# A hybrid decoder layer on one core: h2's first sum alone in the norm's chain, the other sums behind it, and the first gate and up blocks in another order

## The chip, the cores and the metric

One core of a Trainium2 chip runs the whole program. The metric is device microseconds of one launch. The engines are named as in the profile: PE is TensorE (matmuls; PEld its weight loads), DVE is VectorE, ACT is ScalarE, POOL is GpSimd, SP is SyncE, which issues most of the DMAs.

## What is computed

One layer of a decoder with T = 512 tokens and D = 1024, in float32: three token mixers in parallel, their gated sum times `w_out`, a norm and the residual, and then a SwiGLU feed-forward part with DFF = 2816. The change lies where the two meet:

```python
x = x + rmsnorm(mixed @ w_out[l], norm_mix_post[l])
h = rmsnorm(x, norm_ffn_pre[l])
f = (jax.nn.silu(h @ ffn_w_gate[l]) * (h @ ffn_w_up[l])) @ ffn_w_down[l]
x = x + rmsnorm(f, norm_ffn_post[l])
```

The second `h` is called h2 below.

## The kernel before

**Split matmuls.** Each float32 operand is kept as a high part H (a copy by ScalarE that rounds) and a low part L (the rest, a subtraction by VectorE). A product of two operands is three matmuls: H with H, H with L, L with H.

**Seven products for eight.** h2 and the weights of gate and up are cut into 2 x 2 quarters (h2: first or second 256 tokens by first or second half of D; a weight: halves of D by halves of its columns). A block of a gate or up result takes seven products instead of eight. Their left operands are the quarters a11, a12 and a22 of h2 and four sums of quarters: s1 = a22 - a21 (with the kernel's signs), s2 from s1 and a11, s4 from s2 and a12, s3 = a11 - a21. Their right operands are quarters and sums of quarters of the weight. The products accumulate into four PSUM banks, pa, pd and pc by name: pa takes a11, s2, s3 and a22 one after the other, pc takes s1 and s4, pd takes a12. In between, `copy` saves the states c11, c12 and c22.

**Blocks.** The columns of DFF stand as 22 tiles of 128, 11 in each half; `chunks` cuts the 11 into six blocks n = 0 to 5, of two tiles each and one in the last. For every n there is a `Block` for gate ("g", ends in silu into `ga`) and one for up ("u", multiplies into `ga`). A product is 24 matmuls of 128x256 (12 in block 5). `first` is the product with a11, `second` with a12, `middle` those with s1, s2, s4 and s3, `last` the one with a22. `first` and `second` need the first 256 tokens alone.

**Weight sums.** For n in `FF_SUMMED` (0, 4 and 5) the sums of quarters are made in DRAM ahead of time: `behind` takes the next job off a list (`todo`), a copy on SP's queue (L180) and then an accumulating DMA on POOL's queue (L181). The jobs of n = 0 come first, then those of the down weights, then those of n = 4 and 5. Two sums of a weight start from another sum, so their copy waits for that sum's accumulate. The other blocks (n = 1, 2, 3) load four raw quarters (`fetch`, L1017) and sum them on VectorE (`plus`, L1030). Every weight operand is then cast by ScalarE (L1042, "wH") and subtracted by VectorE (L1043, "wL").

**Buffers.** Raw weights go through `avail`, three buffers "raw_ff" and, until n = 4, four more named "fraw". Two halves of one slot carry the names "two_...", so a "two_fraw" in a row is one of these.

**The chain to the sums.** The tokens stand in four row tiles t = 0 to 3. For each, `post_norm` adds to the residual x, `pre_norm` makes hn (L303; its factor by a pow on POOL, L280), PE transposes hn (L306, "h2t"), and `put_h2` copies the transposed half to af (L916) and splits it: `Part.put` has ScalarE copy the high part (L904) and VectorE subtract the low one (L905). With t = 2 and 3, the second 256 tokens, `sums_h2` (L931 to L938) makes all five parts s1, s2, s3, a22 and s4 of that row tile, 128x512 each, at once. The chain of the last two row tiles runs in high priority.

**Order.** A scheduler orders the instructions of each engine by the place in the program and by `tc.high_priority`; weights (loads, casts, sums) are moved ahead by LEAD = 400. Block 0 runs `first` and `second` of gate and up; block 1 of gate likewise (L1133 on), and then the `middle` of g0, of u0, and what is left. So six products stand ahead of the first one with s1. `a11.put` and `a12.put` (L981, L982) split the finished `ga` of a group of tiles for the down projection.

## Time and profile before

| | us |
|---|---|
| runs shown | 836.03, 837.03, 838.95 |
| median | 837.03 |
| profiled execution, its time | 835.83 |
| its span | 833.9 |
| PE busy | 805.1 (97%) |
| DVE busy | 553.2 (66%) |
| ACT busy | 387.4 (46%) |
| POOL busy | 110.3 (13%) |

The profile's times count from the span's start; the span is the part of an execution in which an instruction runs, 1.9 us less than the time. Busy time is the time in which at least one instruction of an engine runs. Matmuls overlap in the rows of a timeline: a row shows when a matmul starts and how long it is in the engine, and the next starts before it ends. "[3.04 <-DVE h2s L905]" behind a row says that the engine was idle for 3.04 us before it and that the instruction at L905 that wrote h2s released it. PEclk is the clock granted to PE, as a share of full speed.

### The profile page before, as it was taken

The page shows a single profiled execution, that of the slowest core. Times are in us where ns is not written, and L with a number is a line of the kernel's source. Part 1 is how long each engine was busy: PE and PEld are TensorE (multiplying, and loading weights), DVE is VectorE, ACT ScalarE, POOL GpSimd, SP SyncE. Part 2 cuts the span into 40 slices and gives each one's busy share as a digit, 9 for nine tenths or more (in the row PEclk, how much of TensorE's full clock was granted, in tenths as well). Part 3 has the DMA queues.
Part 4 walks back from the last instruction along what each step waited for, and adds up shares of the span by engine and source line. Part 5 has one row for each costly group of instructions (what it writes and reads, how often), then busy time and mean ns, then how long its engine had stood idle before and what let it go on. Part 6 is the DMA issues. An engine that isn't in the chain of part 4 may idle for free.

```text
span 833.9 us, 12187 instructions
## 1 busy us (share of the span) xinstructions
PE 805.1 (97%) x4778; PEld 716.4 (86%) x4778; DVE 553.2 (66%) x792; ACT 387.4 (46%) x588; POOL 110.3 (13%) x109
## 2 busy tenths in 40 slices
PE   5999999999999999999999999899999999989995
PEld 5888998889888877888888889899999999778884
DVE  4639967776477644433455685779787756987666
ACT  5445324555365432323343484255545544655552
POOL 2210023211111002322221000100000000000001
PEclk9999999999999999999999999899999999999998
DMA  8574557662776985998756368975730554566772
GB/s 303 151 153 109 144 158 167 159 158 66 205 200 130 295 231 127 251 217 221 190 155 177 119 209 207 263 175 142 193 109 27 162 155 140 187 193 235 219 259 106
DMA packets 114811, 147.35 MB, mean 177 GB/s; under 512 B 5425, under 2 KB 89154, under 8 KB 114370
## 3 DMA queue, kind: packets, MB, share of 16 engines
q1 hardware_dynamic: 96066, 124.56, 46.8%
q0 software_dynamic: 18688, 22.02, 17.8%
q8 instruction: 37, 0.61, 0.3%
q14 instruction: 20, 0.16, 0.1%
HBM read 142.36 MB, written 48.23 MB: 229 GB/s over the span
## 4 chain that ended last, share of the span: by engine, by line
PE 88%; DVE 5%; DMA 3%; ACT 1%; issue 1%; SPq 0%; POOL 0%; DVEq 0%; POOLq 0%; ACTq 0%
PE p L1186 9%; PE paffn_w_up L1049 7%; PE paffn_w_gate L1049 7%; PE pga L244 5%; PE pgb L244 5%; PE pgc L244 5%; PE ow L255 5%; PE pcffn_w_up L1049 3%; PE pcffn_w_gate L1049 3%; PE mv L255 3%; PE gv L255 3%; PE pya L244 3%; PE mq L244 3%; PE pu L244 3%; PE pyb L244 3%; PE mk L244 3%
## 5 line engine op out<-in xcount | busy, mean ns | idle before, releaser
L1178 DVE TENSOR_TENSOR wL_p<-raw_p,wH_p 128x1024 fp32r<-128x1024 f32 (+1 forms) x42 | 47.2, 1131 | 21.3 <-ACT wH_p L1177 21.1
L1177 ACT CAST wH_p<-raw_p 128x1024 fp32r<-128x1024 f32 (+1 forms) x42 | 41.0, 980 | 41.2 <-PE p L1186 13.8
L1186 PE MATMUL p<-wH_p,qs 128*128 128x512 f32 x176 | 54.7, 390 | 0.3 <-ACT two_c_u L1241 0.3
L1186 PE MATMUL p<-wH_p,a 128*128 128x512 f32 x132 | 41.3, 392 | 2.6 <-ACT wH_p L1177 2.6
L181 POOL DMA_DIRECT2D sum_d<-in_ffn_w_down_dram x24 | 21.3, 887 | 156.0 <-DMA sum_d<-in_ffn_w_down_dram 87.6
L1043 DVE TENSOR_TENSOR wL_ffn_w_up<-raw_ff,wH_ffn_w_up 128x1024 fp32r<-128x1024 f32 (+1 forms) x26 | 28.1, 1080 | 19.4 <-ACT wH_ffn_w_up L1042 19.3
L1186 PEld LDWEIGHTS p<-wH_p,qs 128*128 128x128 f32 x176 | 33.0, 188 | 7.5 <-ACT two_c_u L1241 0.7
L1042 ACT CAST wH_ffn_w_up<-raw_ff 128x1024 fp32r<-128x1024 f32 (+1 forms) x26 | 24.2, 932 | 32.6 <-issue 9.1
L1049 PE MATMUL pcffn_w_gate<-h2s,wH_ffn_w_gate 128*128 128x256 f32 x176 | 33.9, 291 | 3.0 <-DVE h2s L905 3.0
L280 POOL TENSOR_TENSOR rs_pf<-ms_pf,half 128x1 f32<-128x1 f32 x4 | 3.7, 921 | 231.7 <-DVE ssq_pf L277 224.0
L1186 PE MATMUL p<-wL_p,qs 128*128 128x512 f32 x88 | 34.2, 389 | 0.0
L1049 PE MATMUL paffn_w_up<-h2s,wH_ffn_w_up 128*128 128x256 f32 x176 | 33.9, 292 | 0.0
L1049 PE MATMUL paffn_w_gate<-h2a,wH_ffn_w_gate 128*128 128x256 f32 x176 | 33.3, 287 | 0.0
L1049 PE MATMUL paffn_w_up<-h2a,wH_ffn_w_up 128*128 128x256 f32 x176 | 32.9, 284 | 0.4 <-DVE c22ffn_w_up L1085 0.4
L1049 PE MATMUL paffn_w_gate<-h2s,wH_ffn_w_gate 128*128 128x256 f32 x176 | 32.8, 284 | 0.2 <-DVE h2s L905 0.2
L1042 ACT CAST wH_ffn_w_gate<-raw_ff 128x1024 fp32r<-128x1024 f32 (+1 forms) x26 | 24.2, 935 | 18.5 <-PE paffn_w_up L1049 6.5
L181 POOL DMA_DIRECT2D sum_ffn_w_gate<-in_ffn_w_gate_dram x12 | 12.5, 1038 | 152.9 <-DMA sum_ffn_w_gate<-sum_ffn_w_gate 86.6
L1049 PE MATMUL pcffn_w_up<-h2s,wH_ffn_w_up 128*128 128x256 f32 x176 | 32.4, 283 | 0.0
L1186 PEld LDWEIGHTS p<-wH_p,a 128*128 128x128 f32 x132 | 24.6, 188 | 8.4 <-ACT wH_p L1177 3.5
L1049 PEld LDWEIGHTS pcffn_w_gate<-h2s,wH_ffn_w_gate 128*128 128x128 f32 x176 | 28.7, 199 | 3.2 <-DVE h2s L905 3.2
L1043 DVE TENSOR_TENSOR wL_ffn_w_gate<-raw_ff,wH_ffn_w_gate 128x1024 fp32r<-128x1024 f32 (+1 forms) x26 | 27.7, 1076 | 4.4 <-ACT wH_ffn_w_gate L1042 4.2
L1042 ACT CAST wH_ffn_w_gate<-two_fraw 128x1024 fp32r<-128x1024 f32 x16 | 16.8, 1048 | 28.5 <-DVE two_fraw L1030 13.0
(406 smaller groups left out, 2647.3 us busy)
## 6 DMA issues: line engine op xcount, KB each, us to landing
sum_d<-in_ffn_w_down_dram POOLq DMA_DIRECT2D x20, 512.0 KB, 7.5
raw_p<-sum_d SPq DMA_DIRECT2D x20, 512.0 KB, 4.1
raw_p<-in_ffn_w_down_dram SPq DMA_DIRECT2D x15, 512.0 KB, 3.7
raw_ff<-in_ffn_w_gate_dram SPq DMA_DIRECT2D x12, 512.0 KB, 4.6
sum_d<-in_ffn_w_down_dram SPq DMA_DIRECT2D x10, 512.0 KB, 5.4
sum_d<-sum_d SPq DMA_DIRECT2D x10, 512.0 KB, 5.8
two_fraw<-in_ffn_w_up_dram SPq DMA_DIRECT2D x10, 512.0 KB, 4.8
sum_ffn_w_gate<-in_ffn_w_gate_dram POOLq DMA_DIRECT2D x8, 512.0 KB, 7.1
```

The lines of the kernel that those rows point to most:

```text
L181: nc.gpsimd.dma_start(dst, second, accum_op=ALU.add)
L244: PE.matmul(ps, lhsT=w[:, k, f * P:(f + 1) * P], rhs=m(k0 + k, lo, hi), start=n == 0 and i == 0, stop=n == len(W) - 1 and i == len(seq) - 1)
L255: PE.matmul(ps, lhsT=m(k0 + k, lo, hi), rhs=w[:, k, c0:c1], start=first and n == 0 and i == 0, stop=last and n == len(W) - 1 and i == len( ...
L280: pows.append(G.tensor_tensor(rs, ms, half[:, 0:1], op=ALU.pow))
L1042: S.copy(h, r)
L1043: V.tensor_tensor(l, r, h.bitcast(F32), op=ALU.subtract)
L1049: PE.matmul(self.ps[b][:, f, :], lhsT=w[:, k, f * P:(f + 1) * P], rhs=X.t[:, z, k, :], start=start and f == 0 and k == 0 and n == 0, stop= ...
L1177: S.copy(h, w)
L1178: V.tensor_tensor(l, w, h.bitcast(F32), op=ALU.subtract)
L1186: PE.matmul(ps[j], lhsT=X.part(z, k, j), rhs=w_[:, k - lo_, :], start=start and k == 0 and i == 0, stop=k == KH - 1 and i == 2, skip_group ...
```

## The change

- **Sums of h2.** `sums_h2` makes s1 alone, per row tile. The sums s2, s4, s3 and the part a22 come in `more_sums_h2`, called once behind the loop over the row tiles and without its priority, each for all 256 tokens (128x1024).
- **More in front.** In block 1 `first` and `second` of up run too before the first product with s1: eight products instead of six. There are six extra raw buffers instead of four; two are given back ahead of n = 4.
- **Alternation.** `middle` becomes a generator `steps`, with a stop behind each product. The steps of g0 and u0 run in turn, then those of g1 and u1 (g1 one ahead).
- **Sums of block 4.** `FF_SUMMED` loses 4, so block 4 loads raw quarters and sums on VectorE. `last` takes one job off the list per block, not two.
- **Banks.** PSUM banks are taken from a list and given back (pd behind `second`, pa and pc behind `last`) instead of turning.
- **a12.** The puts of a12's first two groups stand behind block 5 instead of behind blocks 1 and 3.

```diff
-FF_SUMMED = (0, 4, 5)
+FF_SUMMED = (0, 5)
...
     def sums_h2(c):
-        a11, a12, a21, a22 = (af[i, j][:, :, c * P:(c + 1) * P] for i in range(2) for j in range(2))
         if c == 0:
-            for n in ("s1", "s2", "s3", "a22", "s4"):
-                part[n] = Part(f"h2{n}")
+            part["s1"] = Part("h2s1")
             af["s"] = slot([P, 4, TH], "h2fs")
-        s_ = af["s"][:, :, c * P:(c + 1) * P]
+        a21, a22, s_ = (af[i][:, :, c * P:(c + 1) * P] for i in ((1, 0), (1, 1), "s"))
         V.tensor_tensor(s_, a22, a21, op=ALU.subtract)
         part["s1"].put(s_, c)
+
+    def more_sums_h2():
+        a11, a12, a21, a22 = (af[i, j] for i in range(2) for j in range(2))
+        s_ = af["s"]
+        for n in ("s2", "s4", "s3", "a22"):
+            part[n] = Part(f"h2{n}")
         V.scalar_tensor_tensor(s_, s_, -1.0, a11, ALU.mult, ALU.subtract)
-        part["s2"].put(s_, c)
+        part["s2"].put(s_)
+        V.scalar_tensor_tensor(a12, s_, -1.0, a12, ALU.mult, ALU.subtract)
+        part["s4"].put(a12)
         V.tensor_tensor(a21, a11, a21, op=ALU.subtract)
-        part["s3"].put(a21, c)
-        part["a22"].put(a22, c)
-        V.scalar_tensor_tensor(a12, s_, -1.0, a12, ALU.mult, ALU.subtract)
-        part["s4"].put(a12, c)
+        part["s3"].put(a21)
+        part["a22"].put(a22)
...
+    more_sums_h2()
     free("xr_0", "xr_2", "wn", "h2f00", "h2f01", "h2f10", "h2f11", "h2fs")
...
-    more = [slot([P, 4, 2 * P], f"fraw{i}") for i in range(4)]
+    more = [slot([P, 4, 2 * P], f"fraw{i}") for i in range(6)]
...
+    banks = list(range(8))
...
             if start:
-                self.ps[b] = ff_bank(f"{b}{self.name}").rearrange("p (f t) -> p f t", f=2)[:, 0:self.nf, :]
+                self.bank[b] = banks.pop(0)
+                self.ps[b] = (bank(self.bank[b], f"{b}{self.name}")
+                              .rearrange("p (f t) -> p f t", f=2)[:, 0:self.nf, :])
...
         def middle(self, then):
+            for _ in self.steps(then):
+                pass
+
+        def steps(self, then):
             self.plus((0, 0), (0, 1))
             self.product((0, 0), part["s1"], "pc", True, 1)
             self.c22 = self.copy("pc", "c22")
+            yield
             self.plus((0, 0), (1, 1))
             self.product((0, 0), part["s2"], "pa", False, 2)
             self.c12 = self.copy("pa", "c12")
+            yield
...
         def last(self, then):
             self.plus((0, 0), (1, 0))
             self.product((0, 0), part["a22"], "pa", False, 4)
             then(1, 0, self.ps["pa"], 1.0)
+            banks.extend((self.bank["pa"], self.bank["pc"]))
             self.release()
-            for i in range(2):
-                behind(self.load)
+            behind(self.load)
...
-        if n == FF_SUMMED[1]:
+        if n == 4:
+            avail[:] = raws + more[:4]
+            free("fraw4", "fraw5")
+        if n == FF_SUMMED[-1]:
             avail[:] = raws
             free(*[f"fraw{i}" for i in range(4)])
...
         if n == 1:
-            g.loads((0, 0), (1, 0))
-            g.first()
-            g.second(gt)
+            for b, then in ((g, gt), (u, ut)):
+                b.loads((0, 0), (1, 0))
+                b.first()
+                b.second(then)
             (g0, gt0), (u0, ut0) = pairs[0, "g"], pairs[0, "u"]
-            g0.loads((0, 1), (1, 1))
-            g0.middle(gt0)
-            u0.loads((0, 1), (1, 1))
-            u0.middle(ut0)
+            for _ in zip(g0.steps(gt0), u0.steps(ut0)):
+                pass
             g0.last(gt0)
             u0.last(ut0)
             g.loads((0, 1), (1, 1))
-            g.middle(gt)
-            u.loads((0, 0))
-            u.first()
+            gs, us = g.steps(gt), u.steps(ut)
+            next(gs)
+            u.loads((0, 1), (1, 1))
+            for _ in zip(us, gs):
+                pass
+            for _ in us:
+                pass
             g.last(gt)
-            u.loads((0, 1), (1, 1), (1, 0))
+            u.last(ut)
...
         if hi in (4, 8):
             a11.put(lo // 4, quarter(0, 0, lo // 4))
-            a12.put(lo // 4, quarter(0, 1, lo // 4))
+        if n == FF_SUMMED[-1]:
+            for i in range(2):
+                a12.put(i, quarter(0, 1, i))
```

On PE, the first matmuls of the products from gate block 1's a12 to the last one with s2. The names tell the bank (pc...), the part of h2 (h2s1) and the weight. Before:

```order
L1049 MATMUL pdffn_w_gate1_4300<-h2a12_3739,wH_ffn_w_gate1_4296 128x256 x2
...
L1049 MATMUL pcffn_w_gate0_4332<-h2s1_4056,wH_ffn_w_gate0_4327 128x256 x2
...
L1049 MATMUL paffn_w_gate0_4140<-h2s2_4057,wH_ffn_w_gate0_4359 128x256 x2
...
L1049 MATMUL pcffn_w_up0_4457<-h2s1_4056,wH_ffn_w_up0_4452 128x256 x2
L1049 MATMUL pcffn_w_gate0_4332<-h2s4_4060,wH_ffn_w_gate0_4390 128x256 x2
```

And now:

```order
L1052 MATMUL pdffn_w_gate1_4290<-h2a12_3739,wH_ffn_w_gate1_4286 128x256 x2
...
L1052 MATMUL paffn_w_up1_4323<-h2a11_3738,wH_ffn_w_up1_4319 128x256 x2
...
L1052 MATMUL pdffn_w_up1_4354<-h2a12_3739,wH_ffn_w_up1_4350 128x256 x2
...
L1052 MATMUL pcffn_w_gate0_4386<-h2s1_4056,wH_ffn_w_gate0_4381 128x256 x2
...
L1052 MATMUL pcffn_w_up0_4418<-h2s1_4056,wH_ffn_w_up0_4413 128x256 x2
...
L1052 MATMUL paffn_w_gate0_4130<-h2s2_4102,wH_ffn_w_gate0_4445 128x256
```

Two products of block 1 stand ahead of the first one with s1 now, and gate and up use a part one after the other.

On VectorE, from hn of the last row tile to the last low part of s1 (the second row with h2s1). Before, with eight rows left out, four weights of 128x1024 and four instructions of 128x512:

```order
L303 SCALAR_TENSOR_TENSOR two_hn_f3_4093<-two_h2fs_4061,rs_f3_4100,wn_3672 128x512 x2
L905 TENSOR_TENSOR h2a22_4059<-two_h2f10_4048,h2a22_4059 128x4x128
L905 TENSOR_TENSOR h2s1_4056<-two_h2fs_4061,h2s1_4056 128x4x128
L905 TENSOR_TENSOR h2s3_4058<-two_h2f10_4048,h2s3_4058 128x4x128
...
L931 TENSOR_TENSOR two_h2fs_4061<-two_h2f10_4048 128x4x128
L938 SCALAR_TENSOR_TENSOR two_h2f00_3819<-two_h2fs_4061,two_h2f00_3819 128x4x128
...
L905 TENSOR_TENSOR h2a22_4059<-two_h2f10_4048,h2a22_4059 128x4x128
L905 TENSOR_TENSOR h2s2_4057<-two_h2fs_4061,h2s2_4057 128x4x128
...
L905 TENSOR_TENSOR h2s1_4056<-two_h2fs_4061,h2s1_4056 128x4x128
```

And now, whole:

```order
L303 SCALAR_TENSOR_TENSOR two_hn_f3_4078<-two_h2fs_4057,rs_f3_4085,wn_3672 128x512 x2
L1044 TENSOR_TENSOR wL_ffn_w_gate1_4256<-two_fraw0_4120,wH_ffn_w_gate1_4255 128x1024
L1073 TENSOR_TENSOR c11ffn_w_gate0_4155<-c11ffn_w_gate0_4155,pdffn_w_gate0_4162 128x512
L905 TENSOR_TENSOR h2s1_4056<-two_h2fs_4057,h2s1_4056 128x4x128
L1044 TENSOR_TENSOR wL_ffn_w_gate1_4287<-two_fraw2_4121,wH_ffn_w_gate1_4286 128x1024
L1044 TENSOR_TENSOR wL_ffn_w_up1_4320<-two_fraw2_4121,wH_ffn_w_up1_4319 128x1024
L929 TENSOR_TENSOR two_h2fs_4057<-two_h2f10_4048 128x4x128
L1073 TENSOR_TENSOR c11ffn_w_up0_4219<-c11ffn_w_up0_4219,pdffn_w_up0_4226 128x512
L941 TENSOR_TENSOR two_h2f10_4048<-two_h2f00_3819,two_h2f10_4048 128x1024
L905 TENSOR_TENSOR h2a22_4105<-two_h2f10_4048,h2a22_4105 128x1024
L1119 TENSOR_TENSOR ga00_4123<-c11ffn_w_up0_4219,ga00_4123 128x2x256
L1044 TENSOR_TENSOR wL_ffn_w_up1_4351<-two_fraw4_4122,wH_ffn_w_up1_4350 128x1024
```

The next row is the last low part of s1. The first row tile's s2, s3, a22 and s4 are gone from the stretch; a sum and a part at full width (L941, h2a22) and up1's weights have come in.

On SP's queue, behind the load of up0's third summed weight. Before:

```order
L1017 DMA raw_ff2_4130<-sum4_ffn_w_gate0_1675 128x4x256
L180 DMA sum2_ffn_w_gate4_4607<-sum1_ffn_w_gate4_3572 16x8192
L180 DMA sum2_ffn_w_up4_4610<-sum1_ffn_w_up4_3635 16x8192
L1017 DMA two_fraw0_4131<-sum4_ffn_w_up0_1718 128x4x256
L180 DMA sum4_ffn_w_gate4_4643<-sum2_ffn_w_gate4_4607 16x8192
L1017 DMA two_fraw2_4132<-in_ffn_w_gate_dram 128x4x256
L180 DMA sum4_ffn_w_up4_4646<-sum2_ffn_w_up4_4610 16x8192
L1017 DMA raw_ff0_4128<-in_ffn_w_gate_dram 128x4x256
```

And now:

```order
L1018 DMA raw_ff2_4119<-sum4_ffn_w_gate0_1675 128x4x256
L180 DMA sum2_ffn_w_gate5_4661<-sum1_ffn_w_gate5_3572 16x4096
L1018 DMA two_fraw0_4120<-sum4_ffn_w_up0_1718 128x4x256
L180 DMA sum2_ffn_w_up5_4694<-sum1_ffn_w_up5_3635 16x4096
L1018 DMA two_fraw4_4122<-in_ffn_w_gate_dram 128x4x256
L1018 DMA raw_ff0_4117<-in_ffn_w_gate_dram 128x4x256
L1018 DMA raw_ff1_4118<-in_ffn_w_up_dram 128x4x256
L180 DMA sum4_ffn_w_gate5_4979<-sum2_ffn_w_gate5_4661 16x4096
L1018 DMA raw_ff2_4119<-in_ffn_w_up_dram 128x4x256
L180 DMA sum4_ffn_w_up5_5012<-sum2_ffn_w_up5_4694 16x4096
```

The copy of a sum4 starts from a sum2, whose accumulate it waits for. It stood ahead of the raw loads of block 1 and now stands behind three of four, and its size is half.

## Rows read from the trace of the kernel before

**Rows 1.** The page: busy time by engine; PE's granted clock in 40 slices.

```profile
PE 805.1 (97%) x4778; PEld 716.4 (86%) x4778; DVE 553.2 (66%) x792; ACT 387.4 (46%) x588; POOL 110.3 (13%) x109
...
PEclk9999999999999999999999999899999999999998
```

**Rows 2.** Waits of PE: who waits <- for whom: us in all, times, longest.

```profile
PE paffn_w_gate L1049 <- DVE wL_ffn_w_gate L1043: 3.3, 1, 3.3
PE pcffn_w_gate L1049 <- DVE h2s L905: 3.0, 1, 3.0
```

**Rows 3.** Windows: stretch, length; PE, PEld, DVE, ACT, POOL busy; PEclk, DMA share, GB/s.

```profile
480.00:490.00 10.00, 10.00 (x87) 10.00 (x85) 8.38 (x14) 7.90 (x15) 2.08 (x2) 1.00 0.93 317
490.00:500.00 10.00, 8.34 (x71) 8.14 (x69) 10.00 (x15) 9.55 (x15) 0.00 (x0) 1.00 0.34 96
500.00:510.00 10.00, 8.37 (x55) 8.17 (x56) 8.13 (x11) 4.27 (x7) 0.00 (x0) 0.83 0.70 224
520.00:530.00 10.00, 6.67 (x45) 6.47 (x45) 5.80 (x6) 2.58 (x3) 2.16 (x3) 0.81 0.97 256
540.00:550.00 10.00, 10.00 (x86) 10.00 (x85) 7.12 (x7) 4.76 (x6) 0.00 (x0) 1.00 0.77 224
```

**Rows 4.** Windows over later stretches of gate and up, same columns.

```profile
570.00:650.00 80.00, 80.00 (x668) 79.86 (x666) 65.61 (x66) 41.65 (x51) 4.13 (x4) 1.00 0.40 101
650.00:690.00 40.00, 40.00 (x336) 40.00 (x335) 23.42 (x26) 20.03 (x26) 0.00 (x0) 1.00 0.57 169
```

**Rows 5.** Timeline of PE at stop one: start, us, engine, line, operation, names, shapes.

```profile
498.06 0.28 PE L1049 MATMUL pcffn_w_gate<-h2s,wH_ffn_w_gate 128*128 128x256 f32 x1
501.38 0.39 PE L1049 MATMUL pcffn_w_gate<-h2s,wH_ffn_w_gate 128*128 128x256 f32 x1 [3.04 <-DVE h2s L905]
...
509.15 0.40 PE L1049 MATMUL pcffn_w_up<-h2s,wH_ffn_w_up 128*128 128x256 f32 x2
```

**Rows 6.** Timeline of PE at stop two.

```profile
523.67 0.28 PE L1049 MATMUL pcffn_w_up<-h2s,wL_ffn_w_up 128*128 128x256 f32 x1
...
527.28 0.58 PE L1049 MATMUL paffn_w_gate<-h2a,wL_ffn_w_gate 128*128 128x256 f32 x1 [3.33 <-DVE wL_ffn_w_gate L1043]
...
538.32 0.40 PE L1049 MATMUL paffn_w_gate<-h2s,wH_ffn_w_gate 128*128 128x256 f32 x2
```

**Rows 7.** Timeline of VectorE, around hn and at both stops.

```profile
488.16 1.41 DVE L303 SCALAR_TENSOR_TENSOR two_hn_f<-two_h2fs,rs_f,wn 128x512 f32<-128x512 f32 x2
489.49 0.68 DVE L905 TENSOR_TENSOR h2a<-two_h2f,h2a 128x512 fp32r<-128x512 f32 x1
...
500.65 0.68 DVE L905 TENSOR_TENSOR h2s<-two_h2fs,h2s 128x512 fp32r<-128x512 f32 x1
501.25 0.68 DVE L905 TENSOR_TENSOR h2s<-two_h2f,h2s 128x512 fp32r<-128x512 f32 x1
...
523.73 1.23 DVE L1030 TENSOR_TENSOR two_fraw<-two_fraw,two_fraw 128x1024 f32<-128x1024 f32 x1 [6.73 <-DMA two_fraw<-in_ffn_w_gate_dram]
...
526.01 1.22 DVE L1043 TENSOR_TENSOR wL_ffn_w_gate<-raw_ff,wH_ffn_w_gate 128x1024 fp32r<-128x1024 f32 x1
```

**Rows 8.** Timeline of the SP queue: the DMAs that it issued.

```profile
479.67 0.59 SPq L1017 DMA_DIRECT2D two_fraw<-sum_ffn_w_gate  x1
...
508.49 0.37 SPq L1017 DMA_DIRECT2D two_fraw<-sum_ffn_w_up  x1
517.74 0.47 SPq L180 DMA_DIRECT2D sum_ffn_w_gate<-sum_ffn_w_gate  x1
518.30 0.53 SPq L1017 DMA_DIRECT2D two_fraw<-in_ffn_w_gate_dram  x1
```

**Rows 9.** Waits of the SP queue, columns as in rows 2.

```profile
SPq L180 <- DMA sum_ffn_w_gate<-in_ffn_w_gate_dram: 8.9, 1, 8.9
```

**Rows 10.** DMA issues of 470 to 500: size of each, us from issue to landing.

```profile
two_fraw<-sum_ffn_w_gate SPq DMA_DIRECT2D x1, 512.0 KB, 7.8
```

**Rows 11.** Timeline of PE: the first transposes of the last row tile.

```profile
490.60 0.60 PE L306 MATMUL h2t<-ident,two_hn_f 128*128 128x128 f32 x4
```

## The prediction: the rows put together

> **What bounds the kernel now.** I read the page's busy table first, then TensorE's waits, then windows, then timelines of the places found. TensorE (PE) is busy 97% of the span and its granted clock is full nearly everywhere [rows 1]: only gaps and slow stretches on PE can be won. Outside the program's start, the list of PE's waits has two of more than 3 us, both in the gate/up stage: 3.3 us on a weight's low part (wL, L1043) and 3.0 us on h2s, a sum of quarters of h2 (L905) [rows 2]. The windows give the second half of the cost: in the two stretches that begin with these stops PE was granted 0.83 and 0.81 of full speed, beside 1.00 elsewhere [rows 3]. Since 1.2 and 2.4 GHz are the two levels, each stop is followed by a stretch at half speed.
>
> At the full clock a matmul takes 80.00/668 = 0.12 us [rows 4], so a product of 24 takes 2.88. **Stop one:** the products with s1 and s2 of gate block 0 begin at 498.06, stand 3.04 us after the first matmul, and the product behind them begins at 509.15 [rows 5]. 48 matmuls at 0.12 are 5.76, they took 11.09: **5.33 us lost**, 3.28 of it up to the matmul that had waited, 2.05 the clock. **Stop two:** the last matmul ahead of it ends at 523.67 + 0.12 = 523.79, PE then stands 3.33 us, and the next product but two begins at 538.32 [rows 6]. Between lie 22 + 24 + 24 = 70 matmuls (the PE order), 8.40 at the full clock; they took 14.53: **6.13 us lost**, 3.33 of it standing, 2.8 the clock. From there PE's windows are full at clock 1.00 [rows 3, 4].
>
> Why they stand. Stop one: VectorE is busy 10 of 10 us before it [rows 3]. The low part of s1's second row tile is the row at 500.65 [rows 7], and in the VectorE order four weights and seven instructions of the other sums and parts stand between hn and it. Stop two: VectorE itself stood 6.73 us, up to 523.73, at a weight sum (L1030) for want of a raw load of gate block 1; the weight that PE waits for is the row at 526.01, two places behind in the same queue [rows 7]. That load was issued by the SP queue at 518.30. SP had issued nothing but one load at 508.49 and then stood until 517.74 [rows 8], 8.9 us of it for one DMA accumulate [rows 9]: the copy of a pre-summed n=4 weight waited for its partner, and the load stood behind the copy.
>
> **The change, part by part.**
>
> *Two more half blocks in front (u1's pa and pd).* No matmul is added; 48 x 0.12 = 5.76 us of work move ahead of the first use of s1, which is wanted at 498.06 + 5.76 = 503.82. Cost 0 if their weights are there. The last of today's four early loads was issued at 479.67 [rows 8] and landed 7.8 us later [rows 10], 487.5; at the 317 GB/s of that window [rows 3] two more of 512 KB take 3.3, so the sixth lands near 490.8. Its product begins 2.88 behind today's 498.06, 10 us later. Hidden.
>
> *s1 alone in the chain.* In the new VectorE order, between hn (done 489.49 today) and s1's last low part stand 6 instructions of 128x1024 and 6 of 128x512, that last one among them. Start to start these take 1.14 (two in 526.01 - 523.73) and 0.60 (501.25 - 500.65) [rows 7]: 6.84 + 3.60 = 10.44, so s1 is complete by 499.9, 3.9 us before it is wanted. Stop one goes: **-5.33**.
>
> *The other sums behind it, whole width.* What is late next is s2. Behind s1 stand 7 of 128x1024 and 2 of 128x512, s2's low part last: 7.98 + 1.20 = 9.2, done by 509.1. PE, having done s1 for gate and up (5.76), wants it at 509.58 plus one matmul, 509.7. The margin is 0.6 us, and 1.9 if hn comes 1.3 earlier: a weight and an add, 1.14 + 0.60, that stand right ahead of it in VectorE's queue today stand behind it now, and only GpSimd's pow, which makes its factor, is left to wait for. I take 0, with 0 and +2 as ends; s4 is done 2.9 later, for a use 5.76 later.
>
> *Transposes of the last row tile.* They move 17 matmuls (2.0 us) forward on PE, from 490.60 [rows 11] to 488.56. hn starts at 488.16 today [rows 7] and its first half takes 0.7. If it came no earlier, PE would stand some 0.9 us; the weight and the add no longer ahead of it speak for none. I take 0, ends 0 and +0.9.
>
> *Gate and up alternating.* Same matmuls; each s part serves two products in a row, so PE asks for a new part every 5.76 us instead of 2.88. VectorE owes per such pair one low part, one sum and two weights, 4 x 1.14 = 4.6. Cost 0.
>
> *n=4 no longer pre-summed, one job per block.* SP's queue loses the copies of n=4; those of n=5, of half the size, stay. In the new SP order three loads of block 1 stand ahead of the copy that can wait for an accumulate; behind it stands only u1's fourth quarter, which PE wants some 14 us later. The loads of stop two are then issued near 513 instead of 518.30, land near 518, and the weight of 526.01 is done near 521, for a use that moves from 524 to 527. Stop two goes: **-6.13**. In exchange VectorE makes n=4's weight sums, 8 x 1.14 = 9.1 us, and two a12 puts, 2 x 1.14 = 2.3, move to the end of n=4. VectorE is busy 23.4 of the 40 us of that stretch; 23.4 + 11.4 = 34.8, 87%. The 80 us ahead of it, whose blocks sum on VectorE already, run at 65.6 of 80, 82%, without a gap on PE [rows 4]. So 0, with 0 and +2 as ends.
>
> *Banks as a list, six extra raw buffers.* A bank that is handed out again was emptied several products before. 0.
>
> **Sum:** -5.33 - 6.13 = -11.46. The profiled execution took 835.83 and so would take 824.4; the median of the runs is 837.03, 1.2 above it, so I forecast **825.6 us**.
>
> **Rivals.**
>
> *B, s2 is late.* VectorE has no idle time from 488 on, and 2 us of added delay (a cast on ScalarE or a landing late) use the margin up. PE then stands for the excess, 1 to 3 us, and a stop of 3 also costs the clock some 2.05 to 2.8, as the two stops did: 826.6 to 830.9. For it: the margin of 0.6. Against: hn earlier. Chance 0.13.
>
> *C, stop two stays.* The loads of block 1 are still late, behind an accumulate that takes longer than today's 8.9 us. Only -5.33: 831.7. Chance 0.07.
>
> *D, slower.* VectorE cannot make n=4's sums beside its weights. Place: the 40 us of 650 to 690 today; it decides if a sum comes later than the weights already made ahead. Fully exposed, 11.4 us of gaps in about four stops with some 2.4 us of half clock each: 825.6 + 11.4 + 9.6 = 846.6. 87% asked for beside a gapless 82% [rows 4] speaks against it. Chance 0.05.
>
> *E, the clock under alternating products.* If the turns between PSUM banks cost PE its clock, the 20 alternating products (480 matmuls, 57.6 us) would run at 1.2 instead of 2.4 GHz, up to twice as long: 883. The trace speaks against it: in 540 to 550, where the order has PE turn between three banks, once after two matmuls, PE is busy 10.00 at clock 1.00 [rows 3]. The Trainium skill, "TensorE: Matmul & The Clock Gate", section "A second HAM failure mode: psum-queue depth-cycling", tells of a kernel whose cycling through banks left PE idle for short times so often that its clock went up and down; by that rule this change would lose time. The trace does not agree so far: turns left no gap. Chance 0.02.
>
> **How the numbers follow.** Forecast A 0.72, B 0.13, C 0.07, D 0.05, E 0.02, and 0.01 for no effect. A's own spread is 823.5 to 827.5: the runs of before lie within 2.9 us of each other, and the bounds of the transposes add 0.9. The range 823.5 to 830.5 takes in nearly all of A and B, about 0.83. 0.3% is 2.5 us, about what a measurement of this kernel can tell from no change: A, B and C are faster than 834.5, 0.92; 0.02 within; D and E, with a little rounding, 0.06 slower.
>
> **What would show it.** Right: PE's waits lose both rows of 3 us and name no h2s and no wL above 1 us there; the clock reads 1.00 in every window from 490 to 560; VectorE stays at 10 of 10 around 490 to 511; SP has no wait of 9 us at a copy; PE is full until the turn to the down projection, which begins 11 us earlier. Wrong: a PE wait on h2s2 (B), on a weight of block 1 or on g0's last (C), gaps in n=4 (D), a low clock without a gap before it (E).

## The result and the profile after

The changed kernel took 826.47 us (median of 4 runs, 826.17 to 829.77), the kernel before beside it 836.53 (median of 4). The ratio is 0.9887, with a 95% interval of 0.9851 to 0.9924: faster by about 10 us. The forecast was 825.6, in a range of 823.5 to 830.5. A second set of runs gave 826.50 beside 835.43, a ratio of 0.9896 (0.9876 to 0.9915).

The profiled execution took 829.77 us (span 827.7), the slowest of the four. The page's busy line and PE's clock, to be read beside [rows 1]:

```profile
PE 802.8 (97%) x4778; PEld 713.4 (86%) x4778; DVE 558.6 (67%) x793; ACT 386.0 (47%) x584; POOL 101.0 (12%) x101
...
PEclk9999999999999999999999999999999999989998
```

PE's waits of over 1 us; the answer to [rows 2]:

```profile
PE tp_m L360 <- DVE two_wpre L357: 9.1, 1, 9.1
PE p L1206 <- ACT wH_p L1197: 3.0, 1, 3.0
PE paffn_w_gate L1052 <- DVE c22ffn_w_gate L1096: 1.7, 1, 1.7
```

Both rows of over 3 us in gate and up are gone; the first row here is the program's start. Two others stand in the list: 1.7 us on c22, which is in block 0, and 3.0 us in the down projection.

The windows answer [rows 3, 4] (stretch, length, busy time of PE, PEld, DVE, ACT, POOL, then PEclk, DMA share, GB/s):

```profile
490.00:500.00 10.00, 10.00 (x86) 10.00 (x85) 10.00 (x13) 9.62 (x13) 0.00 (x0) 1.00 0.21 76
500.00:510.00 10.00, 10.00 (x86) 10.00 (x85) 10.00 (x11) 6.91 (x9) 0.00 (x0) 1.00 0.49 157
...
520.00:530.00 10.00, 8.32 (x68) 8.04 (x68) 9.22 (x11) 4.80 (x6) 1.01 (x1) 1.00 1.00 274
...
640.00:680.00 40.00, 40.00 (x336) 40.00 (x335) 33.57 (x34) 21.95 (x28) 0.00 (x0) 1.00 0.12 34
```

PE is busy 20.00 of 20 us and at clock 1.00 where stop one was. In 520 to 530 it lacks 1.68 us, but the clock is 1.00. Block 4 (640 to 680) runs without a gap, with VectorE at 33.57 of 40.

For all that follows, **the gate/up stage** is the time from the first matmul of gate block 0 with a11 to the last matmul of gate and up, both starts read from PE's timeline. Before it lasted 715.18 - 479.06 = 236.12 us, and 833.9 - 715.18 = 118.72 lay behind it. After it lasts 705.57 - 478.99 = 226.58, and 827.7 - 705.57 = 122.13 lie behind it. The first and the last row of the stage, before and then after:

```profile
479.06 0.40 PE L1049 MATMUL paffn_w_gate<-h2a,wH_ffn_w_gate 128*128 128x256 f32 x2
...
715.18 0.28 PE L1049 MATMUL paffn_w_up<-h2a,wL_ffn_w_up 128*128 128x256 f32 x1
```

```profile
478.99 0.40 PE L1052 MATMUL paffn_w_gate<-h2a,wH_ffn_w_gate 128*128 128x256 f32 x2
...
705.57 0.28 PE L1052 MATMUL paffn_w_up<-h2a,wL_ffn_w_up 128*128 128x256 f32 x1
```

So in the two profiled executions the stage gave 9.54 us, and 3.41 were lost again behind it, in the down projection and what follows.

### The profile page after: what moved, and what is told of

It is laid out like the page before. It is cut to its first block, busy times and chain, and to the rows that moved or that the text cites. A ratio compares the mean times of both kernels' runs of the same rounds, so it can differ in the third digit from the quotient of the medians.

```text
span 827.7 us, 12133 instructions
## 1 busy us (share of the span) xinstructions
PE 802.8 (97%) x4778; PEld 713.4 (86%) x4778; DVE 558.6 (67%) x793; ACT 386.0 (47%) x584; POOL 101.0 (12%) x101
## 4 chain that ended last, share of the span: by engine, by line
PE 89%; DVE 4%; DMA 3%; issue 1%; ACT 1%; POOL 0%; SPq 0%; DVEq 0%; POOLq 0%; ACTq 0%
PE p L1206 10%; PE paffn_w_gate L1052 7%; PE paffn_w_up L1052 7%; PE pga L244 5%; PE pgb L244 5%; PE ow L255 5%; PE pgc L244 5%; PE pcffn_w_gate L1052 3%; PE pcffn_w_up L1052 3%; PE mv L255 3%; PE gv L255 3%; PE pya L244 3%; PE mq L244 3%; PE pu L244 3%; PE pyb L244 3%; PE mk L244 3%
## 5 line engine op out<-in xcount | busy, mean ns | idle before, releaser
L1198 DVE TENSOR_TENSOR wL_p<-raw_p,wH_p 128x1024 fp32r<-128x1024 f32 (+1 forms) x42 | 47.2, 1131 | 22.8 <-ACT wH_p L1197 22.5
L1206 PE MATMUL p<-wH_p,a 128*128 128x512 f32 x132 | 43.4, 409 | 3.0 <-ACT wH_p L1197 3.0
L1043 ACT CAST wH_ffn_w_gate<-raw_ff 128x1024 fp32r<-128x1024 f32 (+1 forms) x23 | 20.9, 919 | 29.1 <-DVE raw_ff L1031 11.0
L1043 ACT CAST wH_ffn_w_up<-two_fraw 128x1024 fp32r<-128x1024 f32 x22 | 23.1, 1049 | 21.1 <-issue 5.7
L1044 DVE TENSOR_TENSOR wL_ffn_w_up<-two_fraw,wH_ffn_w_up 128x1024 fp32r<-128x1024 f32 x22 | 26.9, 1221 | 7.7 <-ACT wH_ffn_w_up L1043 7.6
L1052 PEld LDWEIGHTS paffn_w_gate<-h2a,wH_ffn_w_gate 128*128 128x128 f32 x176 | 27.8, 192 | 2.0 <-DVE c22ffn_w_gate L1096 1.9
L1052 PEld LDWEIGHTS paffn_w_up<-h2a,wH_ffn_w_up 128*128 128x128 f32 x176 | 27.6, 192 | 1.0 <-DVE c22ffn_w_up L1096 1.0
L1206 PE MATMUL p<-wL_p,a 128*128 128x512 f32 x66 | 27.0, 410 | 1.0 <-DVE wL_p L1198 0.9
L1052 PEld LDWEIGHTS paffn_w_up<-h2s,wH_ffn_w_up 128*128 128x128 f32 x176 | 27.5, 192 | 0.1
```

Of the source, the lines that this page charges most:

```text
L1043: S.copy(h, r)
L1044: V.tensor_tensor(l, r, h.bitcast(F32), op=ALU.subtract)
L1052: PE.matmul(self.ps[b][:, f, :], lhsT=w[:, k, f * P:(f + 1) * P], rhs=X.t[:, z, k, :], start=start and f == 0 and k == 0 and n == 0, stop= ...
L1198: V.tensor_tensor(l, w, h.bitcast(F32), op=ALU.subtract)
L1206: PE.matmul(ps[j], lhsT=X.part(z, k, j), rhs=w_[:, k - lo_, :], start=start and k == 0 and i == 0, stop=k == KH - 1 and i == 2, skip_group ...
```

## The experiments

The theory was the prediction's: two separate stops. The first is removed by the work in front, the second by freeing SP's queue. The main rivals were that taking s1 alone out of the chain removes the first, that alternating removes it, and that the copies' bytes made the second. The runs were made in sets on different chips, and each ratio is to the kernel before in the same set; runs of different sets compare by their ratios. The changed kernel's own ratios are 0.9887 (0.9851 to 0.9924) and 0.9896 (0.9876 to 0.9915).

### Block 4 and its jobs alone (e1)

The kernel before with this edit, and with a12's first two puts behind block 5 as in the change:

```diff
-FF_SUMMED = (0, 4, 5)
+FF_SUMMED = (0, 5)
...
-            for i in range(2):
-                behind(self.load)
+            behind(self.load)
```

> The kernel before with block 4 summed on VectorE, one job per block and a12's first two puts behind block 5; the order of the products and the sums of h2 are those of before. Theory (stop two comes from the copies in SP's queue, and block 4's sums are covered): stop two goes and stop one stays, so 836.5 - 6.1 = 830.4 us, PE still waits 3.0 us on h2s at L905, and no wait of more than 1 us on a wL of block 0 or 1. Rival (the raw loads are late whatever stands in SP's queue): 836.5, the wait of 3.3 stays. Second rival (block 4's sums are not covered): 840 or more, with gaps on PE between 640 and 690.

Measured: 829.49 us (828.56 to 831.15), ratio 0.9929 (0.9912 to 0.9946), 6.7 below the 836.17 of before. The stage took 230.19, 5.93 less; the prediction had 6.13. PE's timeline still has stop one (3.29 us, 3.04 before), and in SP's issues the copy that waited is gone from ahead of the load:

```profile
501.75 0.38 PE L1049 MATMUL pcffn_w_gate<-h2s,wH_ffn_w_gate 128*128 128x256 f32 x1 [3.29 <-DVE h2s L905]
```

```profile
508.85 0.37 SPq L1017 DMA_DIRECT2D two_fraw<-sum_ffn_w_up  x1
509.32 0.47 SPq L180 DMA_DIRECT2D sum_ffn_w_up<-sum_ffn_w_up  x1
511.98 0.37 SPq L1017 DMA_DIRECT2D two_fraw<-in_ffn_w_gate_dram  x1
```

The raw load of gate block 1 is issued at 511.98 instead of 518.30 [rows 8], and PE has no wait of over 0.3 us between 507 and 705. The second stop is a thing of its own, and block 4's sums cost PE nothing (40.00 of 40 us busy in 640 to 680, as before).

### The new sums alone (e2)

The kernel before with `sums_h2` and `more_sums_h2` of the change, as its diff has them, and nothing else.

> The kernel before with the new sums of h2 alone (s1 alone in the chain, the others behind it at full width), six products in front, gate and up not alternating. Theory (stop one is a matter of how much work stands in front, and s2 is next): s1's last low part is done near 499.4, wanted at 498.06, so PE stands 1.4 instead of 3.0; then s2's low part is done near 508.5 and wanted near 505, a new stop of 3 us. Stop two stays. Time 835 to 840, not below 834. Rival (taking s1 alone is what removes stop one): 836.5 - 5.3 = 831.2.

Measured: 839.71 us (838.65 to 841.6), ratio 1.0051 (1.0034 to 1.0068), 0.5% slower. The stage took 237.92. PE's waits and VectorE's timeline:

```profile
PE paffn_w_up L1054 <- DVE c22ffn_w_up L1090: 7.0, 2, 6.8
...
PE pcffn_w_gate L1054 <- DVE h2s L905: 1.6, 1, 1.6
PE paffn_w_gate L1054 <- ACT h2s L904: 1.4, 1, 1.4
```

```profile
529.10 1.23 DVE L1035 TENSOR_TENSOR two_fraw<-two_fraw,raw_ff 128x1024 f32<-128x1024 f32 x1 [8.25 <-DMA raw_ff<-in_ffn_w_gate_dram]
```

The rearranged sums alone do not remove stop one. They halve it (1.6 where 1.4 was expected) and let s2 come late, by 1.4 instead of the 3 expected; here the wait is for its high part from ScalarE. Stop two grew to 6.8 by the same mechanism in a new guise: SP stood 8.3 us for an accumulate with a raw load of gate block 1 behind it, VectorE stands 8.25 us at a weight sum for that load, and this time c22, which PE needs, is what stands behind it in the queue.

### The old sums in the changed kernel (e3)

The reverse: the change with the `sums_h2` of before, all five sums per row tile.

> The changed kernel with the sums of h2 of before (all five per row tile, in the norm's chain). Theory (the two more products in front are enough for stop one): behind hn (done 488.9) stand 4 instructions of 128x1024 and 12 of 128x512 up to s1's last low part, 4.6 + 7.2 = 11.8, so s1 is done near 500.7 to 501.3 and wanted at 503.8; s2 is done near 508.9 and wanted at 509.6. Time that of the changed kernel within 1.5 us, 825 to 828. Rival (s1 alone is what counts): a stop of 3 us on h2s and its half clock come back, 831 to 832.

Measured: 826.44 us (824.17 to 830.41), ratio 0.9893 (0.9869 to 0.9917), the changed kernel's time. The stage took 226.29. The low part of s1's second tile ran from here,

```profile
501.11 0.69 DVE L905 TENSOR_TENSOR h2s<-two_h2fs,h2s 128x512 fp32r<-128x512 f32 x1
```

and was done at 501.80, half a microsecond later than worked out. PE's first matmul with s1 came at 503.18 and did not wait. Its ratio and the changed kernel's agree within their intervals. So with eight products in front the rearrangement is worth nothing that these runs can show.

### Six products in front (e7), gate and up in turn (e6)

In e7 the change's u1 goes back behind block 0; in e6 the steps no longer alternate:

```diff
-            for b, then in ((g, gt), (u, ut)):
-                b.loads((0, 0), (1, 0))
-                b.first()
-                b.second(then)
+            g.loads((0, 0), (1, 0))
+            g.first()
+            g.second(gt)
...
+            u.loads((0, 0), (1, 0))
+            u.first()
+            u.second(ut)
```

> The changed kernel with u1's two early products back behind block 0, six products in front instead of eight. Theory (the products in front are what removes stop one): s1's last low part is done near 499.4 and wanted at 498.1, a stop of 1.4; s2's is done near 508 and wanted near 505.2, a stop of 2.9; together 4.3 standing and up to 4 of half clock. Gate/up stage 231 to 235, time 830.5 to 835. Rival (the order of the sums alone keeps s1 in time): no wait on h2s of more than 1 us, 826.5.

Measured: 835.08 us (830.17 to 837.46, 12 runs), ratio 0.9986 (0.9968 to 1.0005): nearly all of the gain is gone. The stage took 230.84 in the profiled execution, which is the fastest of the twelve. PE's timeline:

```profile
498.89 0.39 PE L1052 MATMUL pcffn_w_gate<-h2s,wH_ffn_w_gate 128*128 128x256 f32 x1 [1.11 <-DVE h2s L905]
504.88 0.39 PE L1052 MATMUL paffn_w_gate<-h2s,wH_ffn_w_gate 128*128 128x256 f32 x1 [0.21 <-ACT h2s L904]
507.38 0.58 PE L1052 MATMUL pcffn_w_gate<-h2s,wH_ffn_w_gate 128*128 128x256 f32 x1 [1.99 <-ACT h2s L904]
```

Three stops on the sums, 3.3 us, where 4.3 were expected, and PE's clock in 500 to 510 was 0.86. Why most of its other runs were some 5 us slower than the profiled one no trace here shows.

```diff
-            for _ in zip(g0.steps(gt0), u0.steps(ut0)):
-                pass
+            g0.middle(gt0)
+            u0.middle(ut0)
...
-            for _ in zip(us, gs):
-                pass
+            g.middle(gt)
```

> The changed kernel with gate and up of blocks 0 and 1 one after the other instead of alternating. Theory (alternating only buys s2 and s4 2.9 us each): s1 is in time as before; s2's low part is done near 508.6 and wanted near 506.7 now, a stop of about 1.9 us on h2s, without a long stretch at half clock. Gate/up stage 228 to 230, time 827.5 to 830.5. Rival (alternating is what removes stop one): a stop of 3 us or more on h2s and a stretch at half clock, 831 or more. Second rival (it does nothing): 826.5, no wait on h2s.

Measured: 828.70 us (827.79 to 830.46), ratio 0.9924 (0.991 to 0.9938); stage 229.96. PE's timeline:

```profile
507.74 0.39 PE L1052 MATMUL paffn_w_gate<-h2s,wH_ffn_w_gate 128*128 128x256 f32 x1 [1.49 <-DVE h2s L905]
526.25 0.39 PE L1052 MATMUL paffn_w_gate<-h2a,wL_ffn_w_gate 128*128 128x256 f32 x1 [0.85 <-DVE wL_ffn_w_gate L1044]
534.81 0.39 PE L1052 MATMUL pcffn_w_gate<-h2s,wL_ffn_w_gate 128*128 128x256 f32 x1 [2.54 <-DVE wL_ffn_w_gate L1044]
```

Alternating buys 2.2 us by the medians of the two kernels in this set (826.50 for the changed one, see e5; the single runs overlap) and 3.4 to 4.7 us in the stage. The difference lies behind the stage, where this run took 118.71 us beside 121.21 and 122.13 in the two profiles of the changed kernel. The stop on s2 was expected at 1.9 and is 1.5; the 2.5 us on a weight of block 1 was not expected. Its windows from 490 to 560 are all at clock 1.00, and so are those of the alternating kernel: the turns between banks cost no clock that these windows show, and the rival of the clock falls.

### Block 4 pre-summed again (e4)

The change with `FF_SUMMED = (0, 4, 5)` and two jobs per block. The bytes and accumulates are back; but in this order both raw loads of gate block 1 stand ahead of the first copy that waits.

> The changed kernel with block 4 pre-summed in DRAM again and two jobs per block. In its SP order both raw loads of gate block 1 stand ahead of the first copy that waits for an accumulate. Theory (it is the wait in SP's queue that made stop two, not the bytes): stop two does not come back whole; the loads of block 1 land 1 to 3 us later beside copies of twice the size, so the 1.7 us wait on c22 grows by 1 to 3: 827 to 830. Rival (the copies' bytes or the accumulates make the stop): stop two comes back with its half clock, 826.5 + 4 to 6 = 830.5 to 832.5.

Measured: 828.94 us (826.84 to 829.96), ratio 0.9916 (0.9899 to 0.9932). The time lies in the theory's range, but not for its reason: in the profile the stage took 225.68, 0.9 less than in the first profile of the changed kernel, and block 0's wait on gate's c22 is not there. The part behind took 120.63. So the bytes did not bring stop two back, which is what the run was to tell: the load of gate block 1 was issued at 511.81, ahead of the copies that wait. It also means that in the new order stop two stays away with block 4 pre-summed; dropping those copies is what removes it in the old order (e1), and is not needed for it in the new one. Whether the pre-sums cost anything else stays open: the ratio's interval overlaps the changed kernel's, and the one profiled execution is the fastest of the six.

### The changed kernel again (e5), block 5's jobs later (e8)

> The changed kernel unchanged, for a second profile of it. In the first one the gate/up stage (first matmul with a11 of gate block 0 to the last matmul of gate and up) took 226.6 us and the part behind it 122.1. Theory: the stage is the same within 1 us, with a wait of 1 to 2 us on c22; the part behind it varies, 118 to 122, with a stop of 2 to 3 us at the third down product and its half clock in some executions and not in others. Time 824 to 830. Rival (the 3 us between the runs come from the gate/up stage): the stage differs by 2 us or more.

Measured: 826.50 us (824.34 to 829.34). The second profile (827.36) has a stage of 225.30, so 1.28 less than the first, a little more than allowed; the wait on c22 is 0.8 instead of 1.7, and the part behind took 121.21. Both profiles show the same chain. VectorE in the first one:

```profile
520.78 1.23 DVE L1031 TENSOR_TENSOR two_fraw<-two_fraw,two_fraw 128x1024 f32<-128x1024 f32 x1 [3.08 <-DMA two_fraw<-in_ffn_w_gate_dram]
...
528.26 0.68 DVE L1096 TENSOR_TENSOR c22ffn_w_gate<-c22ffn_w_gate,paffn_w_gate 128x512 f32<-128x512 f32 x1
```

and in the second:

```profile
519.34 1.23 DVE L1031 TENSOR_TENSOR two_fraw<-two_fraw,two_fraw 128x1024 f32<-128x1024 f32 x1 [1.84 <-DMA two_fraw<-in_ffn_w_gate_dram]
...
527.05 0.68 DVE L1096 TENSOR_TENSOR c22ffn_w_gate<-c22ffn_w_gate,paffn_w_gate 128x512 f32<-128x512 f32 x1
```

VectorE stands at the first weight sum of block 1, and c22 of gate block 0, eight places behind, comes late by what it stood. PE needs c22 to be read out of pa before the product with a22 adds to pa. The load in the first profile, its issue and then its size and the us to landing:

```profile
513.74 0.43 SPq L1018 DMA_DIRECT2D two_fraw<-in_ffn_w_gate_dram  x1
```

```profile
two_fraw<-in_ffn_w_gate_dram SPq DMA_DIRECT2D x1, 512.0 KB, 7.0
```

In the second profile it was issued at 513.15 and took 6.2. In e8 no copy or accumulate runs beside it:

```diff
-            behind(self.load)
+            if self.key[1] > 1:
+                behind(self.load)
```

> The changed kernel with block 5's last jobs behind blocks 2 and 3 instead of 0 and 1, so that no copy and no accumulate runs beside the loads of block 1. Theory (the new wait of 1.7 us on c22 comes from VectorE standing 3.1 us for a load of block 1 that took 7.0 us beside them): the load lands 1 to 2 us earlier, the wait on c22 falls below 1 us, gate/up stage 225 to 226, time 825 to 826. Rival (the load is late for its buffer, not for the copies): the wait stays at 1.4 to 1.7.

Measured: 826.90 us (824.82 to 828.46), ratio 0.9900 (0.9883 to 0.9916). The load took 5.1 us, VectorE stood 1.22, the wait on c22 was 0.5 and the stage took 225.09:

```profile
519.17 1.22 DVE L1031 TENSOR_TENSOR two_fraw<-two_fraw,two_fraw 128x1024 f32<-128x1024 f32 x1 [1.22 <-DMA two_fraw<-in_ffn_w_gate_dram]
```

All four numbers go the way that was expected, but the cause isn't shown. The unchanged kernel's second profile already had 6.2, 1.84, 0.8 and 225.30, so in the last three most of the step from the first profile came without any edit. And in e4, with copies of twice the size beside it, the load took 5.8 us. What makes this load take 5 to 7 us stays open; that the wait on c22 follows what VectorE stands at that sum holds in all three profiles. The time is not below the changed kernel's. The part behind took 120.77 us, with a stop of 2.9 in it.

### What the down projection gives back (e9, e10)

The first down products in PE's timeline, before and then after, only the rows that waited:

```profile
718.64 0.50 PE L1186 MATMUL p<-wL_p,a 128*128 128x512 f32 x1 [0.42 <-DVE wL_p L1178]
727.68 0.74 PE L1186 MATMUL p<-wH_p,a 128*128 128x512 f32 x2 [0.55 <-ACT wH_p L1177]
745.37 0.74 PE L1186 MATMUL p<-wH_p,a 128*128 128x512 f32 x2 [2.10 <-ACT wH_p L1177]
```

```profile
721.60 0.50 PE L1206 MATMUL p<-wL_p,a 128*128 128x512 f32 x1 [0.50 <-DVE wL_p L1198]
725.00 0.50 PE L1206 MATMUL p<-wL_p,a 128*128 128x512 f32 x1 [0.40 <-DVE wL_p L1198]
736.92 1.22 PE L1206 MATMUL p<-wH_p,a 128*128 128x512 f32 x2 [3.04 <-ACT wH_p L1197]
```

And the window of the long stop after the change, whose clock is 0.90 (before, the window with the 2.10 was at 1.00):

```profile
720.00:740.00 20.00, 15.96 (x60) 11.82 (x59) 18.47 (x18) 10.63 (x12) 0.00 (x0) 0.90 0.65 174
```

VectorE is nearly full there, with weights, parts and sums for all down products. The stop of 3.04 can be followed back to it. The weight that PE waits for is cast by ScalarE at 735.82, which had stood 4.32 us for its load; SP issued that load at 730.39, having waited for a buffer that VectorE's subtraction of an earlier weight, at 729.15, gives back:

```profile
729.15 1.21 DVE L1198 TENSOR_TENSOR wL_p<-raw_p,wH_p 128x1024 fp32r<-128x1024 f32 x1
...
730.39 0.37 SPq L1215 DMA_DIRECT2D raw_p<-sum_d  x1
...
735.82 1.04 ACT L1197 CAST wH_p<-raw_p 128x1024 fp32r<-128x1024 f32 x1 [4.32 <-DMA raw_p<-sum_d]
```

Three sums that only the sixth product needs were given to GpSimd in e9:

```diff
-        V.tensor_tensor(quarter(1, 0, i), quarter(0, 0, i), quarter(1, 0, i), op=ALU.subtract)
+        G.tensor_tensor(quarter(1, 0, i), quarter(0, 0, i), quarter(1, 0, i), op=ALU.subtract)
```

> The changed kernel with the three sums for the product p7 (L1256) made by GpSimd instead of VectorE. In both profiles of the changed kernel the part behind gate and up takes 121 to 122 us beside 118.7 before, with one stop of 2.8 to 3.0 at the third down product and a clock of 0.90 to 0.91 behind it, where before it was split in 0.4, 0.6 and 2.1 at full clock. Theory (VectorE's queue is the bound of that turn): 1.14 + 1.14 + 0.87 = 3.1 us leave VectorE's queue, the stop falls below 2 us and the clock stays full, the part behind takes 117 to 119, time 823 to 825. Rival (the loads are the bound): the stop stays at 2.8 or more, 826.5. Second rival (GpSimd's sums slow VectorE beside them): VectorE's 128x1024 rows stretch and the time is 826.5 or more.

Measured: 824.01 us (823.58 to 824.73), ratio 0.9859 (0.9839 to 0.9879), the lowest ratio with e10; its interval still touches the changed kernel's. The stop on wH is gone from PE's list; what is left are three of at most 1.6 us on weights of the down projection, and the clock is 1.00 in every window from 700 to 760. The same chain runs 3.5 us earlier (2.7 counted from the start of the gate/up stage):

```profile
725.66 1.22 DVE L1198 TENSOR_TENSOR wL_p<-raw_p,wH_p 128x1024 fp32r<-128x1024 f32 x1
...
726.90 0.37 SPq L1215 DMA_DIRECT2D raw_p<-sum_d  x1
...
732.19 1.05 ACT L1197 CAST wH_p<-raw_p 128x1024 fp32r<-128x1024 f32 x1 [4.13 <-DMA raw_p<-sum_d]
```

From the load's issue to the cast it takes 5.3 us, beside 5.4 in the changed kernel; what moved is the moment at which VectorE lets the load start. PE takes down products between those of gate and up more than before in this version, so the mark at the last gate/up matmul (708.92) doesn't compare; from the first one to the span's end it took 821.9 - 478.16 = 343.7 us, beside 348.7 and 346.5 in the two profiles of the changed kernel.

> As the run before, and the eight weight sums of block 1 made by GpSimd too. Theory (the wait on c22 comes from weight sums that stand for their load ahead of c22 in VectorE's queue): no wait on c22 of block 0 above 0.3 us, gate/up stage 224 to 225, time 822.5 to 824. Rival (GpSimd is too slow for them, 2.5 us for 128x1088 in the one row of it beside VectorE's 1.14): PE waits for a weight of block 1, 826 or more.

In e10 `plus` of block 1 uses GpSimd too. Measured: 823.91 us (823.46 to 825.23), ratio 0.9863 (0.9843 to 0.9884): no better. The waits in the stage are all at most 0.4 us, but no gain came of it, and GpSimd's sums were not free; see below.

## Why the prediction was right, and where a size was off

**Stop one, -5.33: right, and for the stated reason.** s1's last low part was worked out to be done by 499.9 and wanted at 503.82. In the trace it starts at 498.75 and is done at 499.43; PE's first matmul with s1 is at 503.75 and doesn't wait. VectorE's rows of s1 and s2, and PE's first rows that need them:

```profile
498.75 0.68 DVE L905 TENSOR_TENSOR h2s<-two_h2fs,h2s 128x512 fp32r<-128x512 f32 x1
...
507.36 1.21 DVE L905 TENSOR_TENSOR h2s<-two_h2fs,h2s 128x1024 fp32r<-128x1024 f32 x1
```

```profile
503.75 0.40 PE L1052 MATMUL pcffn_w_gate<-h2s,wH_ffn_w_gate 128*128 128x256 f32 x2
...
509.51 0.28 PE L1052 MATMUL paffn_w_gate<-h2s,wH_ffn_w_gate 128*128 128x256 f32 x1
```

The runs e2, e3 and e7 say which part does it: the two more products in front. The prediction costed the work in front as the thing that moves the demand, and the sums as the thing that moves the supply; the second was not needed. Its split of the 5.33 is off, without effect on the sum: [rows 5] give 501.38 - 498.06 - 0.12 = 3.20 up to the matmul that had waited, not 3.28, and the rest is not the clock alone. The trace of before has a second wait of 0.24 us on h2s, at the product with s2 (506.30).

**s2, the margin of rival B: held.** It was to be done by 509.1 and wanted at 509.7; it was done at 508.57, and PE came to it at 509.51 and a matmul later. What alternating adds is shown by e6: without it s2 is late by 1.5 us.

**The transposes: 0, as taken.** hn started 0.56 us earlier than before (487.60), and PE's transposes ran at 488.49 without a wait.

**Stop two, -6.13: right in cause.** e1 gave 5.93 in the stage by this part alone, and e4 that it was the wait in SP's queue and not the copies' bytes. In the full change it was over-sized, and in the stage this is the one term that was off. The prediction had the load of block 1 issued near 513 and landed near 518. It was issued at 513.74 and landed 7.0 us later, and VectorE stood 3.08 us at the sum that needed it. The prediction had followed only the weight that PE wanted in the old order, g0's with a22, and found it in time. It had not asked what else stands behind that sum in VectorE's queue, and there it was c22: 1.68 us in one profile, 0.79 in the other. That wait stands on g0's last, the sign that the prediction had named for rival C; it came in small, though SP's longest wait at a copy was 3.5 us and not 8.9, and the load was not behind it. In the stage, -11.46 was forecast, and -9.54 and -10.82 were measured.

**Block 4's sums, 0: right.** 34.8 of 40 us were worked out for VectorE and 33.57 measured, with no gap on PE. e1 shows it by itself, and rival D falls.

**Behind the stage: not foreseen.** The prediction took the down projection as unchanged. Both profiles of the changed kernel have it 2.5 to 3.4 us longer than the one of before, with one stop of 2.8 to 3.0 at the third product and half clock behind it. The stop hangs on VectorE's queue: e9, which takes three sums out of it, loses the stop. But e3's profile, with the same stage, has its longest stop there at 1.67 and 117.69 us behind it. The order that the scheduler gave VectorE differs: of the three sums that e9 moves, the second runs at 704.29 in e3, ahead of the last gate and up matmul, and at 716.59 in the changed kernel, behind it. So a change 200 us earlier can alter that turn. That this order alone makes the difference, and which part of the change brought it, no run shows; e3's profiled execution is also the fastest of its six.

The profiled execution was forecast at 824.4 and took 829.77, so it missed by 5.4 us: 1.92 in the stage and 3.41 behind it. The median fits better, 836.53 - 826.47 = 10.06 for 11.46, because the other three runs took 826.17 to 826.62; where they were faster no trace shows.

**Not tried:** a12's puts at their old place, since they hold buffers that block 4's raw weights need now. That the banks and the extra raw buffers cost PE nothing rests on the trace alone, whose list of PE's waits names none for them.

## What to carry to other kernels

When a product waits for a chain, first move work that needs none of it ahead of the product; shortening the chain is the second thing to try, and here it was worth nothing once that was done. A wait in an in-order queue need not be about the instruction that waits, as both stops here show: list what stands behind it, and for each item who wants it and when, since removing one victim promotes the next (the a22 weight, then c22). And after a gain of one per cent read the stages behind the change too, by marks in the timeline, since the scheduler may have laid them out anew, as it did here.

## What the hardware showed that was not expected

**GpSimd beside a busy VectorE.** In e9 the first GpSimd sum of 128x1024 took 2.78 us, and two VectorE subtractions of 128x512 beside it 3.24, where the same two took 1.30 in e5. The second, of the same size, took 22.5 us in a stretch where VectorE was busy nearly all the time; VectorE's rows of 128x1024 there stayed at 1.21 to 1.22 up to 733. Around the start of the third, of 128x768 (734.8, 2.85 us), two VectorE rows of 128x1024 took 2.69 and 2.87. In e10 weights beside GpSimd's sums are stretched from 1.22 to as much as 4.01 us:

```profile
522.27 2.59 POOL L1031 TENSOR_TENSOR two_fraw<-two_fraw,raw_ff 128x1024 f32<-128x1024 f32 x1 [0.22 <-DMA raw_ff<-in_ffn_w_gate_dram]
```

```profile
522.51 3.43 DVE L1044 TENSOR_TENSOR wL_ffn_w_up<-two_fraw,wH_ffn_w_up 128x1024 fp32r<-128x1024 f32 x1
...
532.04 4.01 DVE L1044 TENSOR_TENSOR wL_ffn_w_up<-two_fraw,wH_ffn_w_up 128x1024 fp32r<-128x1024 f32 x1
```

So the first sum of e9 cost VectorE 1.94 us by these rows and saved it 1.14; the other two together cost it 3.12 and saved it 2.01, although for most of the second's 22.5 us no VectorE row was stretched. That e9 gained all the same fits the chain above, in which what counts is when one subtraction of VectorE ends, not how much it does in all; no run here separates the two.

**Which stops cost the clock.** The stop of 3.04 us in the down projection was followed by a stretch at the lower of the two levels, and so were those of 2.83 and 2.90 in the profiles of e5 and e4. That of 2.93 in e2's and that of 2.54 in e6's were not (1.00). In e7 a stop of 1.99, behind two of 1.11 and 0.21 in the 10 us ahead of it, was followed by the lower level too. Length alone does not tell them apart here.
